# Latent attention: the queries without rotary part by rows, ahead of the rotary ones, through a DRAM round trip

## The chip, the cores and the metric

One Trainium2 chip, one core of it. The metric is the device time of one execution of the whole program in microseconds; the time before is the median of three runs.

## What is computed

A decoder trunk of four layers on 256 tokens of width 2048, all in float32. Layers 0 and 3 mix tokens by latent attention, layer 1 by sparse attention, layer 2 by a sliding window. Every layer also attends to a memory and multiplies its heads by a SiLU gate. The change touches only the latent layers. Cut to what it touches:

```python
c_q, c_kv, k_rope, mq, gate = _split(h @ w_in, [1536, 512, 64, 1024, 3072])
q  = (_rmsnorm(c_q, q_norm) @ w_uq).reshape(B, S, 16, 128 + 64)
kv = (_rmsnorm(c_kv, kv_norm) @ w_ukv).reshape(B, S, 16, 128 + 128)
q_nope, q_rope = q[..., :128], _rope(q[..., 128:])
k_nope, v = kv[..., :128], kv[..., 128:]
s = (einsum('bqhd,bkhd->bhqk', q_nope, k_nope) + einsum('bqhd,bkd->bhqk', q_rope, _rope(k_rope))) * scale
p = softmax(where(causal, s, -1e30))
o = einsum('bhqk,bkhd->bqhd', p, v)
```

## The kernel before

Products keep float32 accuracy by splitting both factors into a high and a low part (`split`, `parts_of`) and adding three products: high by high, high by low, low by high. ScalarE writes the high part `wh`, VectorE subtracts and writes the low part `wl`; each has three buffers, the raw weights `wr` five, so that weights are split up to two stages ahead of the one that TensorE is using.

There are two forms of projection. `columns_by` holds the weights still and streams the tokens, so that features come out on the partitions: per 128 input features and 256 output features it issues two matmuls of 512 columns and two of 256. `rows_by` holds the tokens still and streams the weights, so that tokens come out on the partitions: per 128 input features and up to 512 output features it issues six matmuls of that many columns. What `rows_by` gives must still be transposed before it can be a factor of the scores. `turned` transposes 32x32 blocks on VectorE, `stored` writes the result to DRAM with one DMA, and `fetched` reads it back with four DMAs that put the blocks in their places; `placed` is the two together, on GpSimd's queue.

A latent layer works in parts. Part 4 is memory heads, then parts 0 to 3 are four heads each, then part 5 is memory heads again. For each of parts 0 to 3 `Latent.project` forms, in this order on TensorE: the rotary queries by rows (`acc_qr`), the queries without rotary part by columns in two halves (`acc_qn`), the keys by columns in two halves (`acc_kn`) and the values by rows (`acc_va`). The rotary queries go from PSUM through `rope` and `turned` into the round trip (`qrT`, `placed`, `qrR`), and are split into two stacked parts (lines 832 and 833) when they are back. The others are split straight out of PSUM by `head_parts`. Then `attend` computes the scores of four heads (`sp`), `gate_by_rows` the gate (`acc_gr`), and `w_out` the output projection of the part before (`acc_wo`). There are eight such parts in the program.

The program is built with `schedule_with_timeline_sim=True`: the order of the instructions in each engine's queue is fixed when it is built, by a list schedule over modelled times, and may differ from the order in the text. `keep_in_program_order(ins)` pins one instruction behind the one traced just before it on its engine. The copy of what a round trip brings back is pinned in this way each time. On the chip every engine works through its queue in order and waits at the first instruction whose inputs are not there.

Tiles share buffers by tag. `pq` has five buffers; a part takes five tiles of it (`qrR`, two `qn`, two `kn`). PSUM has two accumulators `acc` and four small banks `mp`.

Of the kernel before, what the change touches and what calls it, by code (L numbers as in the profile page):

```python
# [8 lines left out]
F32 = mybir.dt.float32  # L9
# [6 lines left out]
P = 128  # L16
# [16 lines left out]
def kernel(ctx: ExitStack, tc: tile.TileContext, a: dict, out: bass.AP,  # L33
# [13 lines left out]
    def tmp(name, n=512, dt=F32):  # L47
        return wk.tile([P, n], dt, name=name, tag=f"t{n}", bufs=3)
# [5 lines left out]
    def f32(ap):  # L54
        return ap.bitcast(F32)

    def copy_act(o, i, scale=1.0):
        return nc.scalar.activation(o, i, AF.Copy, scale=scale)  # L58

    def split(hi, lo, src):  # L60
        copy_act(hi, src)
        nc.vector.tensor_sub(lo, src, f32(hi))  # L62
# [181 lines left out]
    def rows_by(xt, kts, w, k0, cols, name, hooks={}, opening=False, between={}):  # L244

        acc = accumulators(name)
        n = cols[1] if len(cols) == 2 else cols[1] * cols[4]
        step = 4 if n <= 256 else ST
        for s in range(0, kts, step):
            wr, n = stage(w, k0 + s, step, cols)  # L250
            if opening:
                for f in hooks[s]:
                    f()
            wh, wl = parts_of(wr, step * n, n if opening and s < 8 else None)
            with ExitStack() as held:
                for f in between.get(s, ()):
                    ins = f()
                    if ins is not None:
                        held.enter_context(tc.issue_after(ins))
                for k in range(step):  # L260
                    q = xt[(s + k) // 4]
                    at = slice(k * n, (k + 1) * n)
                    for t in range(2):
                        xh, xl = (q[:, v, (s + k) % 4, t * P:(t + 1) * P] for v in range(2))
                        first, last = s + k == 0, s + k == kts - 1
                        nc.tensor.matmul(acc[:, t, :n], xh, wh[:, at], start=first, stop=False)  # L266
                        nc.tensor.matmul(acc[:, t, :n], xh, wl[:, at], start=False, stop=False)  # L267
                        nc.tensor.matmul(acc[:, t, :n], xl, wh[:, at], start=False, stop=last)  # L268
            for f in () if opening else hooks.get(s, ()):
                f()  # L270
        return acc

    def columns_by(xt, kts, w, k0, cols, name, hooks={}, apart=False):

        if apart:
            acc = [misc(f"acc_{name}")[:].rearrange("p (v s) -> p v s", v=2) for j in range(2)]
        else:
            whole = accumulators(name)[:].rearrange("p j (v s) -> p j v s", v=2)
            acc = [whole[:, j] for j in range(2)]
        step = 2 * ST  # L280
        for s in range(0, kts, step):
            wr, n = stage(w, k0 + s, step, cols)
            wh, wl = parts_of(wr, step * n)
            for k in range(step):
                kt = s + k
                q = xt[kt // 4]
                first, last = kt == 0, kt == kts - 1
                at = [slice(k * S + j * P, k * S + (j + 1) * P) for j in range(2)]
                for j in range(2):
                    nc.tensor.matmul(acc[j], wh[:, at[j]], q[:, :, kt % 4, :], start=first, stop=False)  # L290
                for j in range(2):
                    nc.tensor.matmul(acc[j][:, 0, :], wl[:, at[j]], q[:, 0, kt % 4, :],  # L292
                                     start=False, stop=last)
            for f in hooks.get(s, ()):
                f()
        return acc if apart else whole
# [169 lines left out]
    def placed(raw, T, n):  # L466
        fetched(raw, stored(T), n, nc.gpsimd.dma_start)
# [12 lines left out]
    def quads(q):  # L480
        return q.rearrange("p m (t b) -> p m t b", b=32)

    def raw_tile(name):
        return act.tile([P, 1024], F32, name=name, tag="pq", bufs=PQ)
# [249 lines left out]
    class Latent:  # L734
# [76 lines left out]
        def project(self, g, steps):  # L811

            j = self.j
            wq, wkv = a["w_uq"][j], a["w_ukv"][j]
            qn, kn = [], []
            qr = act.tile([P, 4, S], F32R, name="qrT", tag="aux", bufs=AUX)
            v = [act.tile([P, 2, 512], F32R, name="va", tag="aux", bufs=AUX) for z in range(2)]
            acc = rows_by(self.cT[:3], 12, wq, 0, (g * 768, 4, 192, A_NOPE, A_ROPE), "qr",
                          {0: steps[:1], 4: steps[1:3], 8: steps[3:]})
            T, raw = tmp("qrT")[:].rearrange("p (t w) -> p t w", t=2), raw_tile("qrR")  # L820
            for t in range(2):
                rr = wk.tile([P, 4, A_ROPE], F32, name="qrr", tag="e", bufs=4)
                rope(rr, acc[:, t, :S].rearrange("p (h d) -> p h d", h=4), t, 4)
                turned(T[:, t], rr.rearrange("p h d -> p (h d)"), 2)
            placed(raw[:].rearrange("p (t w) -> p t w", t=8), T, 2)
            for half in range(2):
                acc = columns_by(self.cT[:3], 12, wq, 0, (g * 768 + half * 384, 2, 192, 0, A_NOPE), "qn")
                q = act.tile([P, 2, 2, S], F32R, name="qn", tag="pq", bufs=PQ)
                head_parts(q, acc)
                qn.append(q)  # L830
            r4 = raw[:].rearrange("p (t m b) -> p m t b", m=4, b=32)
            tc.keep_in_program_order(copy_act(quads(qr), r4))
            nc.vector.tensor_sub(quads(qr)[64:], r4[64:], quads(f32(qr))[64:])
            for half in range(2):
                acc = columns_by(self.cT[3:], 4, wkv, 0, (g * 1024 + half * 512, 2, 256, 0, A_NOPE), "kn",
                                 apart=half == 1)
                k = act.tile([P, 2, 2, S], F32R, name="kn", tag="pq", bufs=PQ)
                head_parts(k, acc)
                kn.append(k)
            acc = rows_by(self.cT[3:], 4, wkv, 0, (g * 1024, 4, 256, A_NOPE, A_NOPE), "va")  # L840
            split(v[0], v[1], acc)
            return (qn, qr, kn, v), lambda: gate_by_rows(self.nm, self.w, self.g0 + g * 512)

        def attend(self, qn, qr, kn, v):
            ws = []
            for h in range(4):
                def score(b):
                    sp = misc("sp")
                    qs = slice(b * P, (b + 1) * P)
                    q, k, z = qn[h // 2], kn[h // 2], h % 2  # L850
                    if b == 0:
                        seq = [(q[:, 0, z, qs], k[:, :, z, :P]), (q[:, 1, z, qs], k[:, :, z, :P]),
                               (qr[:, h, qs], self.kr[:, :, :P])]
                    else:
                        seq = [(q[:, 0, z, qs], k[:, 0, z, :]), (q[:, 0, z, qs], k[:, 1, z, :]),
                               (q[:, 1, z, qs], k[:, 0, z, :]),
                               (qr[:, h, qs], self.kr[:, 0, :]), (qr[:, h, qs], self.kr[:, 1, :])]
                    for n_, (l, r_) in enumerate(seq):
                        nc.tensor.matmul(sp[:, :S], l, r_, start=n_ == 0, stop=n_ == len(seq) - 1)
                    return sp  # L860
                if h % 2 == 0:
                    ws.append(Turn(2, CAUSAL))
                ws[-1].add(h % 2, masked_softmax(score, lambda b, n, u: caus[:, S - n:], self.scale))
                if h % 2 == 1:
                    ws[-1].send()

            def sums(z, y, gT, p_s):
                o = misc("o")
                pp = [p_.rearrange("p (t n b) -> p t n b", t=12, n=2) for p_ in p_s[0]]
                for s in range(2):  # L870
                    c = (2 * z + s) * P
                    for t in range(2):
                        ts = slice(8 * t, 8 + 4 * t)
                        for n_, (u, p_) in enumerate(((0, 0), (0, 1), (1, 0))):
                            nc.tensor.matmul(o[:, s * S + t * P:(s + 1) * S], v[u][:, t, c:c + P],
                                             pp[p_][:, ts, s, :], start=t == n_ == 0, stop=t == 1 and n_ == 2)
                return None, lambda: gated(y, o, gT, 2 * z)
            return Sums([ws[:1], ws[1:]], sums)
# [408 lines left out]
```

## Time and profile before

| | |
|---|---|
| runs, median (lowest to highest) | 2529.37 us (2529.0 to 2533.69) |
| profiled execution, its own time | 2527.35 us |
| its span in the trace | 2525.6 us |
| TensorE busy (PE) | 2507.0 us, 99% |
| VectorE (DVE), ScalarE (ACT), GpSimd (POOL) busy | 72%, 56%, 15% |
| mean granted TensorE clock | 0.999 |

PE is TensorE's matmuls, PEld its weight loads, which overlap them. DMA-issuing instructions are not counted as busy time. A matmul's row gives its start and the time until its result is written; matmuls overlap, so the pace is read from the starts.

### The profile page before, as it was taken

The page shows a single profiled execution, that of the slowest core. Times are in us where ns is not written, and L with a number is a line of the kernel's source. Part 1 is how long each engine was busy: PE and PEld are TensorE (multiplying, and loading weights), DVE is VectorE, ACT ScalarE, POOL GpSimd, SP SyncE. Part 2 cuts the span into 40 slices and gives each one's busy share as a digit, 9 for nine tenths or more (in the row PEclk, how much of TensorE's full clock was granted, in tenths as well). Part 3 has the DMA queues.
Part 4 walks back from the last instruction along what each step waited for, and adds up shares of the span by engine and source line. Part 5 has one row for each costly group of instructions (what it writes and reads, how often), then busy time and mean ns, then how long its engine had stood idle before and what let it go on. Part 6 is the DMA issues. An engine that isn't in the chain of part 4 may idle for free.

```text
span 2525.6 us, 37537 instructions
## 1 busy us (share of the span) xinstructions
PE 2507.0 (99%) x13076; PEld 2150.6 (85%) x13076; DVE 1809.3 (72%) x3047; ACT 1417.7 (56%) x2228; POOL 367.6 (15%) x585
## 2 busy tenths in 40 slices
PE   8999999999999999999999999999999999999998
PEld 6888888888888888988888888888889898888887
DVE  6555556677777675778888775888877667767677
ACT  6454545554555555566666555666665655545554
POOL 1000000111121100012222201222220011111210
PEclk9999999999999999999999999999999999999999
DMA  9888888778778756679989677999975877788874
GB/s 315 264 281 291 268 262 243 211 202 211 216 223 227 212 189 193 199 240 275 261 276 266 208 217 207 271 271 270 258 232 165 241 195 212 208 223 225 244 206 148
DMA packets 462014, 588.85 MB, mean 233 GB/s; under 512 B 78896, under 2 KB 294592, under 8 KB 460672
## 3 DMA queue, kind: packets, MB, share of 16 engines
q1 hardware_dynamic: 424080, 470.76, 63.5%
q0 software_dynamic: 36736, 114.78, 15.7%
q8 instruction: 103, 1.69, 0.3%
q10 hardware_dynamic: 1008, 0.91, 0.1%
q14 instruction: 87, 0.71, 0.1%
HBM read 532.10 MB, written 66.81 MB: 237 GB/s over the span
## 4 chain that ended last, share of the span: by engine, by line
PE 97%; DMA 1%; DVE 1%; ACT 1%; issue 0%; POOL 0%; SPq 0%; ACTq 0%; DVEq 0%; POOLq 0%
PE acc_mq L290 5%; PE acc_g L290 5%; PE acc_gr L266 5%; PE acc_gr L267 5%; PE acc_gr L268 5%; PE acc_wo L268 4%; PE acc_wo L267 4%; PE acc_wo L266 4%; PE acc_cq L290 4%; PE acc_qn L290 3%; PE acc_wo L241 3%; PE acc_wo L239 3%; PE acc_wo L240 3%; PE acc_mq L292 2%; PE acc_g L292 2%; PE acc_mk L267 2%
## 5 line engine op out<-in xcount | busy, mean ns | idle before, releaser
L72 DVE TENSOR_TENSOR wl<-wr,wh 128x1024 fp32r<-128x1024 f32 (+2 forms) x860 | 1027.9, 1197 | 556.0 <-ACT wh L58 542.5
L58 ACT ACTIVATE wh<-wr 128x1024 fp32r<-128x1024 f32 (+2 forms) x860 | 891.3, 1038 | 845.3 <-PE acc_gr L268 96.9
L266 PE MATMUL acc_gr<-wh,xT 128*128 128x512 f32 x512 | 199.7, 390 | 0.0
L267 PE MATMUL acc_gr<-wl,xT 128*128 128x512 f32 x512 | 199.6, 390 | 0.0
L268 PE MATMUL acc_gr<-wh,xT 128*128 128x512 f32 x512 | 199.4, 390 | 0.0
L266 PE MATMUL acc_wo<-wh,y 128*128 128x512 f32 x432 | 168.7, 390 | 0.0
L267 PE MATMUL acc_wo<-wl,y 128*128 128x512 f32 x432 | 168.6, 390 | 0.0
L268 PE MATMUL acc_wo<-wh,y 128*128 128x512 f32 x432 | 168.6, 390 | 0.0
L290 PE MATMUL acc_g<-xT,wh 128*128 128x512 f32 x512 | 162.1, 395 | 0.0
L290 PE MATMUL acc_mq<-xT,wh 128*128 128x512 f32 x512 | 161.9, 396 | 0.0
L577 POOL DMA_DIRECT2D pL<-turn x192 | 120.3, 633 | 195.4 <-DMA turn<-T 86.7
L241 PE MATMUL acc_wo<-wh,y 128*128 128x512 f32 x320 | 125.0, 391 | 0.2 <-DVE y L62 0.2
L239 PE MATMUL acc_wo<-wh,y 128*128 128x512 f32 x320 | 124.9, 390 | 0.0
L240 PE MATMUL acc_wo<-wl,y 128*128 128x512 f32 x320 | 124.8, 390 | 0.0
L1191 DVE TENSOR_TENSOR x<-x,acc_wo 128x1024 f32<-128x1024 f32 x92 | 111.5, 1212 | 16.0 <-PE acc_wo L268 11.8
L572 POOL DMA_DIRECT2D turn<-T x56 | 42.8, 765 | 539.6 <-DVE T L566 472.0
L290 PE MATMUL acc_qn<-cT,wh 128*128 128x512 f32 x384 | 120.6, 395 | 0.0
L290 PE MATMUL acc_cq<-xT,wh 128*128 128x512 f32 x384 | 120.6, 395 | 0.0
L292 PEld LDWEIGHTS acc_g<-xT,wl 128*128 128x128 f32 x512 | 96.0, 188 | 21.7
L292 PEld LDWEIGHTS acc_mq<-xT,wl 128*128 128x128 f32 x512 | 95.2, 188 | 21.2
L268 PEld LDWEIGHTS acc_gr<-wh,xT 128*128 128x128 f32 x512 | 96.2, 188 | 19.6
L266 PEld LDWEIGHTS acc_gr<-wh,xT 128*128 128x128 f32 x512 | 96.3, 188 | 18.8
(337 smaller groups left out, 5791.2 us busy)
## 6 DMA issues: line engine op xcount, KB each, us to landing
wr<-in_w_out_dram SPq DMA_DIRECT2D x192, 512.0 KB, 4.8
wr<-in_w_in_a_dram SPq DMA_DIRECT2D x176, 512.0 KB, 4.6
wr<-in_w_mem_kv_dram SPq DMA_DIRECT2D x128, 512.0 KB, 5.8
wr<-in_w_in_b_dram SPq DMA_DIRECT2D x116, 512.0 KB, 4.7
wr<-in_w_in_c_dram SPq DMA_DIRECT2D x104, 512.0 KB, 5.0
wr<-in_w_uq_dram SPq DMA_DIRECT2D x288, 128.0 KB, 3.7
turn<-T POOLq DMA_DIRECT2D x40, 384.0 KB, 5.0
tab<-flat POOLq DMA_DIRECT2D x8, 1536.0 KB, 11.4
```

What stands on the lines that cost most here:

```text
L58: return nc.scalar.activation(o, i, AF.Copy, scale=scale)
L72: two = nc.vector.tensor_sub(lo, src, f32(hi))
L239: nc.tensor.matmul(accs[c][:, t], xh, wh[:, at], start=first, stop=False)
L240: nc.tensor.matmul(accs[c][:, t], xh, wl[:, at], start=False, stop=False)
L241: nc.tensor.matmul(accs[c][:, t], xl, wh[:, at], start=False, stop=last)
L266: nc.tensor.matmul(acc[:, t, :n], xh, wh[:, at], start=first, stop=False)
L267: nc.tensor.matmul(acc[:, t, :n], xh, wl[:, at], start=False, stop=False)
L268: nc.tensor.matmul(acc[:, t, :n], xl, wh[:, at], start=False, stop=last)
L290: nc.tensor.matmul(acc[j], wh[:, at[j]], q[:, :, kt % 4, :], start=first, stop=False)
L292: nc.tensor.matmul(acc[j][:, 0, :], wl[:, at[j]], q[:, 0, kt % 4, :], start=False, stop=last)
L577: nc.gpsimd.dma_start(f32(self.raw)[j * 32:(j + 1) * 32, :].rearrange("p (i r) -> p i r", r=r), bass.AP(tensor=d.tensor, offset=d.offset + ...
L1191: nc.vector.tensor_add(xs, xs, acc)
```

## The change

In each of the eight parts the queries without rotary part are formed first, by `rows_by` with 512 output features. ScalarE copies them out of PSUM, VectorE transposes them in blocks, and they make the same round trip through DRAM that the rotary queries make. Then come the rotary queries, the keys and the values. The split of the fetched queries (`parts_q`) is traced inside the value projection, that of the rotary queries behind it. The scores read the two parts from two tiles instead of one; their matmuls are the same in number and size. A part now takes seven tiles of tag `pq`, which still has five buffers.

```diff
-            acc = rows_by(self.cT[:3], 12, wq, 0, (g * 768, 4, 192, A_NOPE, A_ROPE), "qr",
+            acc = rows_by(self.cT[:3], 12, wq, 0, (g * 768, 4, 192, 0, A_NOPE), "qn",
                           {0: steps[:1], 4: steps[1:3], 8: steps[3:]})
+            T, qraw = act.tile([P, 2, 512], F32, name="qnT", tag="pq", bufs=PQ), raw_tile("qnR")
+            for t in range(2):
+                rows_ = wk.tile([P, 512], F32, name="qnz", tag="z", bufs=2)
+                copy_act(rows_, acc[:, t])
+                turned(T[:, t], rows_, 4)
+            placed(qraw[:].rearrange("p (t w) -> p t w", t=8), T, 4)
+            acc = rows_by(self.cT[:3], 12, wq, 0, (g * 768, 4, 192, A_NOPE, A_ROPE), "qr")
...
             for half in range(2):
-                acc = columns_by(self.cT[:3], 12, wq, 0, (g * 768 + half * 384, 2, 192, 0, A_NOPE), "qn")
-                q = act.tile([P, 2, 2, S], F32R, name="qn", tag="pq", bufs=PQ)
-                head_parts(q, acc)
-                qn.append(q)
-            r4 = raw[:].rearrange("p (t m b) -> p m t b", m=4, b=32)
-            tc.keep_in_program_order(copy_act(quads(qr), r4))
-            nc.vector.tensor_sub(quads(qr)[64:], r4[64:], quads(f32(qr))[64:])
-            for half in range(2):
                 acc = columns_by(self.cT[3:], 4, wkv, 0, (g * 1024 + half * 512, 2, 256, 0, A_NOPE), "kn",
                                  apart=half == 1)
                 k = act.tile([P, 2, 2, S], F32R, name="kn", tag="pq", bufs=PQ)
                 head_parts(k, acc)
                 kn.append(k)
-            acc = rows_by(self.cT[3:], 4, wkv, 0, (g * 1024, 4, 256, A_NOPE, A_NOPE), "va")
+
+            def parts_q():
+                q = [act.tile([P, 4, S], F32R, name="qn", tag="pq", bufs=PQ) for z in range(2)]
+                r4 = qraw[:].rearrange("p (t m b) -> p m t b", m=4, b=32)
+                tc.keep_in_program_order(copy_act(quads(q[0]), r4))
+                nc.vector.tensor_sub(quads(q[1]), r4, quads(f32(q[0])))
+                qn.extend(q)
+            acc = rows_by(self.cT[3:], 4, wkv, 0, (g * 1024, 4, 256, A_NOPE, A_NOPE), "va", {0: [parts_q]})
             split(v[0], v[1], acc)
+            r4 = raw[:].rearrange("p (t m b) -> p m t b", m=4, b=32)
+            tc.keep_in_program_order(copy_act(quads(qr), r4))
+            nc.vector.tensor_sub(quads(qr)[64:], r4[64:], quads(f32(qr))[64:])
```

## Rows read from the trace of the kernel before

**Rows 1.** The page: its span, and TensorE's busy time.

```profile
span 2525.6 us, 37537 instructions
...
PE 2507.0 (99%) x13076; PEld 2150.6 (85%) x13076; DVE 1809.3 (72%) x3047; ACT 1417.7 (56%) x2228; POOL 367.6 (15%) x585
```

**Rows 2.** Waits of PE: total us, times, longest.

```profile
PE acc_mv L266 <- ACT wh L58: 7.4, 1, 7.4
PE acc_mv L267 <- DVE wl L72: 1.4, 2, 0.7
PE acc_va L266 <- DVE qn L317: 1.1, 2, 0.7
```

**Rows 3.** Timeline of PE, first latent part: start, us, instruction.

```profile
502.83 0.28 PE L266 MATMUL acc_qr<-wh,cT 128*128 128x256 f32 x1
...
511.58 0.63 PE L290 MATMUL acc_qn<-cT,wh 128*128 128x512 f32 x2
...
524.79 0.62 PE L290 MATMUL acc_qn<-cT,wh 128*128 128x512 f32 x2
...
531.06 0.63 PE L290 MATMUL acc_kn<-cT,wh 128*128 128x512 f32 x2
...
536.63 0.40 PE L266 MATMUL acc_va<-wh,cT 128*128 128x512 f32 x1
...
542.10 0.40 PE L859 MATMUL sp<-kn,qn 128*128 128x256 f32 x2
...
557.13 0.39 PE L267 MATMUL acc_gr<-wl,xT 128*128 128x512 f32 x1
...
567.78 0.39 PE L239 MATMUL acc_wo<-wh,y 128*128 128x512 f32 x1
```

**Rows 4.** Tile acc_qn, on DVE: duration ns, least, median, most.

```profile
L317 DVE TENSOR_TENSOR qn<-zl,acc_qn x16: 677/687/689, 524.9 to 2366.1; 128x512 fp32r<-128x512 f32 x16
```

**Rows 5.** Tiles gTt and qrT: the operations nearest to the added ones.

```profile
L457 DVE STREAM_TRANSPOSE gTt<-th x32: 669/705/711, 573.1 to 2406.0; 128x512 f32<-128x512 f32 x32
...
L58 ACT ACTIVATE qrT<-qrR x8: 1051/1052/1061, 532.5 to 2363.7; 128x1024 fp32r<-128x1024 f32 x8
L833 DVE TENSOR_TENSOR qrT<-qrR,qrT x8: 1222/1223/1224, 534.0 to 2364.8; 64x1024 fp32r<-64x1024 f32 x8
```

**Rows 6.** DMA issues: count, KB each, median us from issue to landing.

```profile
qrR<-placed POOLq DMA_DIRECT2D x32, 128.0 KB, 5.4
...
placed<-qrT POOLq DMA_DIRECT2D x8, 256.0 KB, 3.5
...
placed<-ckT POOLq DMA_DIRECT2D x2, 512.0 KB, 5.3
```

**Rows 7.** Timelines of DVE and POOL, first part: the rotary queries' way out.

```profile
516.45 0.45 DVE L457 STREAM_TRANSPOSE qrT<-qrr 128x256 f32<-128x256 f32 x1
...
517.20 0.72 POOL L463 DMA_DIRECT2D placed<-qrT  x1 [17.79 <-DVE qrT L457]
520.75 2.33 POOL L473 DMA_DIRECT2D qrR<-placed  x4 [2.84 <-issue]
```

**Rows 8.** Timelines of ACT, first part, and waits of ACT.

```profile
542.30 1.03 ACT L58 ACTIVATE va<-acc_va 128x1024 fp32r<-128x1024 f32 x1 [1.66 <-PE acc_va L268]
...
ACT wh L58 <- PE acc_gr L268: 96.9, 74, 1.7
```

**Rows 9.** Tile qrT's waits, and POOL, ACT, PE in the second part.

```profile
  DMA qrR<-placed: 3.8, 3
...
612.72 2.42 POOL L473 DMA_DIRECT2D qrR<-placed  x4 [4.68 <-DMA placed<-qrT]
...
620.92 1.06 ACT L58 ACTIVATE qrT<-qrR 128x1024 fp32r<-128x1024 f32 x1 [1.70 <-DMA qrR<-placed]
...
624.10 0.47 PE L266 MATMUL acc_va<-wh,cT 128*128 128x512 f32 x1 [0.65 <-DVE qn L317]
```

**Rows 10.** Timelines of DVE and PE: the attention sums of one part.

```profile
583.82 0.95 DVE L585 TENSOR_TENSOR pL<-pL,pH 128x768 fp32r<-128x768 f32 x1
...
589.72 0.28 PE L875 MATMUL o<-pL,va 128*128 128x256 f32 x1
```

More of the change, by code (lines that the diff above doesn't have):

```diff
@@ L849, in score @@
                     qs = slice(b * P, (b + 1) * P)
-                    q, k, z = qn[h // 2], kn[h // 2], h % 2
+                    (hi, lo), k, z = (u[:, h, qs] for u in qn), kn[h // 2], h % 2
                     if b == 0:
-                        seq = [(q[:, 0, z, qs], k[:, :, z, :P]), (q[:, 1, z, qs], k[:, :, z, :P]),
+                        seq = [(hi, k[:, :, z, :P]), (lo, k[:, :, z, :P]),
                                (qr[:, h, qs], self.kr[:, :, :P])]
                     else:
-                        seq = [(q[:, 0, z, qs], k[:, 0, z, :]), (q[:, 0, z, qs], k[:, 1, z, :]),
-                               (q[:, 1, z, qs], k[:, 0, z, :]),
+                        seq = [(hi, k[:, 0, z, :]), (hi, k[:, 1, z, :]), (lo, k[:, 0, z, :]),
                                (qr[:, h, qs], self.kr[:, 0, :]), (qr[:, h, qs], self.kr[:, 1, :])]
```

## The prediction

> **What bounds the kernel now.** I read the page first, then the waits of TensorE, then the timelines of one latent part. The page shows TensorE busy for 2507.0 of 2525.6 us [rows 1], and the list of its waits shows hardly anything else: 8.8 us in the projection of the memory values, and 1.1 us in two of the eight latent parts [rows 2]. So time can go in two ways only: TensorE is given less work, or it is made to wait. VectorE, ScalarE, GpSimd and the DMA queues matter only through the second.
>
> **What TensorE saves.** I compare the two forms by the distance of their matmuls' starts. By columns, nine blocks of 128 input features for 256 outputs lie between 524.79 and 531.06 us, which is 0.697 us for each [rows 3]. By rows, 47 matmuls of 512 columns lie between 557.13 and 567.78 us, 0.2266 us for each [rows 3]. A part needs 24 blocks by columns, 24 x 0.697 = 16.72 us, or 12 x 6 = 72 matmuls by rows, 72 x 0.2266 = 16.32 us. That is 0.40 us in a part and 3.2 us in eight. The columns streamed are the same; 96 matmuls become 72. The first matmuls of the value projection are slower, 5.47 us for 24 between 536.63 and 542.10 [rows 3], which is 0.228 each; at that pace the saving would be 0.30 a part, 2.4 us. I take 3.2, since before and behind the new stage stands work that is as steady as the gate's, and keep 2.4 as its lower end.
>
> The 1.1 us wait [rows 2] also goes: the value projection waited for an accumulator that `head_parts` on VectorE had not yet emptied, and the accumulator that it takes is now the rotary queries', which `rope` has read before the last transpose ends, 5.3 us behind `acc_qr` [rows 7]; the keys between take 5.57 [rows 3]. Together 4.3 us off 2527.35.
>
> **What costs nothing.** VectorE gives up two subtractions and two additions of 0.69 us a part [rows 4], 2.7 us, and takes on two transposes of 0.70 and one subtraction that I price at the 1.22 us of the rotary one [rows 5], 2.6 us. ScalarE takes on one copy of 1.05 us [rows 5], 8.4 us in all at 56% busy. GpSimd issues five more DMAs a part, at the 0.72 and 2.33 us of the rotary ones [rows 7], 24 us in all at 15% busy. 8 MB more pass through DMA. The weights come in 12 larger loads instead of 24. All of it lies under TensorE's 99%. If that cover were gone, only ScalarE's 8.4 us and GpSimd's 24 us would show.
>
> **What becomes late.** Before, the rotary queries' round trip ran under the whole `acc_qn` stage: from the end of `acc_qr` at 511.58 to the first score at 542.10 are 30.5 us [rows 3]. After, only keys and values lie between: 531.06 to 542.10, 11.0 us [rows 3]. Does the round trip fit?
>
> Counted from the end of `acc_qr`: the second transpose ends at 516.90, +5.3; the store is issued at +5.6 and the fetches from +9.2 [rows 7]. They are four, of 0.58 us each, so the last starts at +10.9, and lands 5.4 us later by the median [rows 6], at +16.3. ScalarE's copy takes 1.05 and VectorE's subtraction 1.22 [rows 5]; with 0.3 us for the two hand-overs the scores can start at +18.9. That is 7.9 us behind the end of the value projection. The second part gives the late side: there the fetches came 0.72 + 4.68 = 5.4 us after the store's start, against 3.6 in the first part, and ScalarE waited for the last of them until 620.92, 8.2 us after 612.72 [rows 9], against my 7.1. That makes 5.6 + 5.4 + 8.2 + 2.6 = +21.8, 10.8 us behind.
>
> On ScalarE the copy stands pinned behind the copy of the values, which ends 1.2 us behind the value projection [rows 3, 8], at +12.3. From there to +16.3 ScalarE waits, and behind it in its queue stand the splits of the gate's next weights. TensorE lives on the weights that are already split. With three buffers and one in use these are two stages, 24 matmuls of 0.2266, 5.4 us. That buffers are what splits wait for, not ScalarE, shows in its waits: 97 us, in 74 pieces, for a gate stage to end [rows 8]. So TensorE runs dry for 7.9 - 5.4 = 2.4 us in each part, 19 us in eight parts. The ends of this term: nothing, if a third gate stage is split in time (8.2 us of cover); (10.8 - 5.4) x 8 = 43 us, if all parts are like the second; 63 us, if the scores were queued directly behind the values, 7.9 x 8.
>
> That a late landing reaches TensorE through ScalarE's queue, the trace shows on a small scale. In three of eight parts the copy waited for the fetch, 3.8 us together; where it waited 1.70 us, TensorE lost 0.65 at the next accumulator, in spite of the longer distance [rows 9].
>
> There is one more coupling. Seven tiles share five `pq` buffers. While the fetched queries, both keys and the two query parts live, all five are taken, so the rotary fetch may have to wait until the subtraction of `parts_q` has freed the fetched tile. Out of PSUM by an estimated +2.5 us behind `acc_qn` (two copies of half of 1.05, a last transpose of 0.70 and hand-overs, from [rows 5]), stored by +7.8 and landed by +15 [rows 6, 7], split by +17.6: with 8.75 us for `acc_qr` between [rows 3], +8.8 on the rotary count, just ahead of +9.2. It adds nothing in the middle case and belongs to the late end.
>
> The sum: 2527.35 - 4.3 + 19 = 2542. The runs' median lies 2.0 us above the profiled execution, so I forecast 2544 us for the median.
>
> **The rivals.** First, the round trip stays hidden. The order of the queue is chosen over modelled times, and TensorE is often given an operand later than it is there: one attention sum starts 5 us after its subtraction has ended [rows 10]. If the scores are queued behind three gate stages or more, and the third stage's split stands ahead of the waiting copy, TensorE never waits and only the saving is left: 2529.4 - 4.3 = 2525. Against it stands that the copy is pinned so that ScalarE arrives at it 4 us too early, however well the rest is ordered.
>
> A rule speaks for this rival. The Trainium skill, page "DMA: Bandwidth & Descriptors", section "Anatomy of one DMA — SWDGE (gpsimd) path", gives a DMA from GpSimd's queue as 2.0 us plus its bytes at 436 GB/s; that would be an estimated 2.6 us for the store and 2.3 for a fetch, data at about +12.5, just when ScalarE comes to it, and a sum of 2525. The trace's medians of 3.5 and 5.4 [rows 6] speak against it.
>
> Second, the queries without rotary part are late as well. `parts_q` is pinned behind the split of the value projection's first weights only. If ScalarE reaches it before the fetch lands at +15, the split of the value projection's second weights waits behind it: 15 + 1.05 + 1.05 + 1.2 = 18.3, where TensorE wants them at 8.75 + 5.57 + 2.73 = 17.0 after `acc_qn` [rows 3, 5]. This adds 1.3 us a part, 10 us in all: 2554. It decides only if that split is not yet made when `acc_kn`'s first half ends.
>
> Third, the scores are queued directly behind the values: 2529 - 4.3 + 63 = 2588. In the trace before they are, but there their inputs were long there.
>
> **How the numbers follow.** A measurement of this kernel can tell about 0.2%, 5 us, from no change. I give 0.52 to the forecast, of which 0.12 is for stalls of under 9 us in all, which would leave the time within 5 us; 0.36 to the first rival; 0.08 to the second; 0.04 to the third. The first rival's 2525 lies 0.8 us from the line of 2524.3, so a good third of it, 0.13, counts as faster and 0.23 as the same. Slower is 0.40 + 0.08 + 0.04 = 0.52, the same 0.12 + 0.23 = 0.35. The forecast's own range, with stalls of 1 to 4.5 us a part, is 2533 to 2561. The range takes in the first rival, down to 2523, and reaches up to 2566, 5 us a part, short of the late end and the third rival.
>
> **What would show it.** Right: `acc_qn` by rows takes 16.3 us a part; ScalarE's list of waits has the rotary copy behind its fetch with 2 to 6 us each, eight times; TensorE's list has `sp` or `acc_gr` with 1 to 4 us each, behind that copy, its subtraction or a weight split. Wrong: no new wait of TensorE, with several gate matmuls between the values and the first score; or waits in `acc_va`, which would be the second rival. The forecast fails if the modelled order leaves 8 us or more of gate work ahead of the first score.

## The result, and the profile after

The changed kernel takes 2549.22 us in the median of four runs (2544.14 to 2551.99), the kernel before 2529.78 beside it: a ratio of 1.0068, 95% interval 1.0055 to 1.0081. By that ratio it is 17 us slower; 2544 was forecast. The profiled execution of the changed kernel took 2544.14 us, with a span of 2542.4, against 2525.6 [rows 1]: 16.8 us more.

The page: span, and busy time of each engine.

```profile
span 2542.4 us, 37010 instructions
...
PE 2509.7 (99%) x12884; PEld 2141.5 (84%) x12884; DVE 1805.0 (71%) x3039; ACT 1419.5 (56%) x2236; POOL 392.0 (15%) x625
```

The waits of PE, which answer to [rows 2] (total us, times, longest):

```profile
PE sp L867 <- DVE kn L317: 13.1, 8, 1.6
PE acc_mv L266 <- ACT wh L58: 7.1, 1, 7.1
PE acc_mv L267 <- DVE wl L72: 1.4, 2, 0.7
PE o L883 <- ACT pH L58: 1.1, 1, 1.1
PE sp L867 <- DVE qn L844: 0.6, 2, 0.4
```

and of ACT and DVE:

```profile
ACT qrT L58 <- DMA qrR<-placed: 39.0, 8, 5.6
...
DVE qrT L850 <- ACT qrT L58: 30.1, 8, 4.5
```

ACT waits for the rotary fetch eight times, 4.9 us on average, as forecast. But PE's new wait stands elsewhere: at the first scores, for the low part of the *keys*. Of what hangs on the rotary fetch, PE's list has only 0.6 us.

The second latent part shows why. The timeline of PE, then ACT, DVE and POOL (start, us, instruction):

```profile
625.54 0.40 PE L266 MATMUL acc_va<-wh,cT 128*128 128x512 f32 x1
...
630.79 0.39 PE L268 MATMUL acc_va<-wh,cT 128*128 128x512 f32 x1
632.81 0.59 PE L867 MATMUL sp<-kn,qn 128*128 128x256 f32 x3 [1.64 <-DVE kn L317]
...
641.81 0.39 PE L266 MATMUL acc_gr<-wh,xT 128*128 128x512 f32 x1
642.62 0.39 PE L867 MATMUL sp<-kn,qn 128*128 128x256 f32 x1 [0.42 <-DVE qn L844]
```

```profile
628.49 1.06 ACT L58 ACTIVATE wh<-wr 128x1024 fp32r<-128x1024 f32 x1 [1.92 <-PE acc_va L268]
629.46 1.12 ACT L58 ACTIVATE kn<-acc_kn 128x512 fp32r<-128x512 f32 x3
...
632.31 1.08 ACT L58 ACTIVATE wh<-wr 128x1024 fp32r<-128x1024 f32 x1
638.99 1.06 ACT L58 ACTIVATE qrT<-qrR 128x1024 fp32r<-128x1024 f32 x1 [5.60 <-DMA qrR<-placed]
...
631.99 0.68 DVE L317 TENSOR_TENSOR kn<-zl,acc_kn 128x512 fp32r<-128x512 f32 x1
...
640.08 1.22 DVE L850 TENSOR_TENSOR qrT<-qrR,qrT 64x1024 fp32r<-64x1024 f32 x1 [4.49 <-ACT qrT L58]
641.34 1.23 DVE L844 TENSOR_TENSOR qn<-qnR,qn 128x1024 fp32r<-128x1024 f32 x1
...
626.16 0.72 POOL L463 DMA_DIRECT2D placed<-qrT  x1 [5.68 <-DVE qrT L457]
630.44 2.46 POOL L473 DMA_DIRECT2D qrR<-placed  x4 [3.56 <-ACT kn L58]
```

The keys are complete in PSUM when the values begin, at 625.54. ACT copies them out at 629.46 only, behind a split of gate weights that itself waits 1.92 us for a buffer. Their low part comes at 632.67 and the first scores at 632.81; the values end at 631.02 (their last start and one pace of 0.2266). That is 1.8 us in each of the eight parts, 14.3 us. Before, the first copy of the keys started 6.8 to 7.3 us ahead of the values' end; now it starts 1.6 ahead. In the kernel before, in the first part, where the values end at 542.10:

```profile
534.78 0.58 ACT L58 ACTIVATE kn<-acc_kn 128x512 fp32r<-128x512 f32 x1
```

The first scores need no rotary part and no low part of the queries. The matmuls that do stand 9.3 us behind the first scores, after 37 gate matmuls (8.4 us) and a few more scores, so the late rotary data (copied from 8.0 us behind the values' end on, split by +10.3) cost little. POOL's row names the keys' copy as what released the fetch, but it is only the last of several: from the store's issue to the first fetch it is 4.3 to 7.2 us in the eight parts, and 3.7 to 7.0 in a later run (`e_aux`) in which the keys are copied much earlier. The last two rows of DVE show a second thing to explain: the low part of the queries without rotary part (L844), whose data were copied to their high part at 630.46, is formed at 641.34, right behind the rotary subtraction (L850).

### The profile page after: what moved, and what is told of

Read it like the earlier page. It is cut to its first block, busy times and chain, and to the rows that moved or that the text cites. A ratio compares the mean times of both kernels' runs of the same rounds, so it can differ in the third digit from the quotient of the medians.

```text
span 2542.4 us, 37010 instructions
## 1 busy us (share of the span) xinstructions
PE 2509.7 (99%) x12884; PEld 2141.5 (84%) x12884; DVE 1805.0 (71%) x3039; ACT 1419.5 (56%) x2236; POOL 392.0 (15%) x625
## 5 line engine op out<-in xcount | busy, mean ns | idle before, releaser
L267 PEld LDWEIGHTS acc_gr<-wl,xT 128*128 128x128 f32 x512 | 96.3, 188 | 18.5
```

## The experiments

Two theories at first. *Rotary*, the prediction's: the fetch is late, and what stands behind it sets the loss. *Keys*: the late copy of the keys is the loss. Times are medians; a ratio is to the kernel before on the same chip. Times "behind the values" are counted from the last `acc_va` matmul's start and one pace.

**The changed kernel again** (`after_again`).

> The changed kernel once more, as the measure for the other three, which run on the same chip. Every theory: 2544 to 2552 us. The profile again shows in each of the 8 parts a gap of about 1.8 us on PE ahead of the first scores (first use of the keys' low part), and ACT waiting some 5 us for the fetch of the rotary queries 8 times.

2550.33 us, ratio 1.0083 (1.0071 to 1.0095). The 13.1 us at the keys come back to the digit. This profiled execution, 2552.00 us, has 5 us more of waits of PE at the attention sums (`o` behind `pH`, the high part of the probabilities) than the first: the 10 us between its runs lie at least partly there.

**Keys first** (`e_kn`). The gate's stages are built inside `issue_after` of the keys' copies.

```diff
+ def gating():
+     with ExitStack() as held:
+         for ins in keys_first:      # head_parts' copies out of PSUM
+             held.enter_context(tc.issue_after(ins))
+         return gate_by_rows(...)
```

> One order is changed: ACT issues the copies of the gate's stages only behind the two copies of the keys out of PSUM. The gap of 1.8 us ahead of the first scores (keys' low part) must go in any case. The keys theory (the late copy of the keys is the loss, 8 x 1.8 = 14 us of it): 2528 to 2534 us, with no new wait on PE. The rotary theory (the prediction's: rotary parts and, in the queue behind them, the queries' low parts are ready some 11.5 us behind the values, and the cover is about 10 us without the gap): the gap moves to the first matmul with the queries' low part, 1 to 2 us in each part, and the time stays at 2538 to 2548 us.

2578.93 us, 1.0197 (1.0174 to 1.0219): worse than either theory said. The gap at the keys is gone. PE's waits now, and the timelines of ACT and PE in the second part:

```profile
PE acc_gr L266 <- ACT wh L58: 15.0, 8, 2.9
PE acc_gr L267 <- DVE wl L72: 8.4, 8, 1.1
```

```profile
643.54 1.06 ACT L58 ACTIVATE qrT<-qrR 128x1024 fp32r<-128x1024 f32 x1 [7.32 <-DMA qrR<-placed]
644.50 2.94 ACT L58 ACTIVATE wh<-wr 128x1024 fp32r<-128x1024 f32 x3
...
645.60 0.49 PE L266 MATMUL acc_gr<-wh,xT 128*128 128x512 f32 x1 [2.47 <-ACT wh L58]
```

This is the prediction's mechanism: ACT stands at the rotary copy, three weight splits stand behind it, PE runs dry, though behind three gate stages (36 matmuls) and not two. In the changed kernel the gap at the keys hides it: there, in the second part, the fourth gate stage starts at 641.81 and its split ends at about 641.0, so without the 1.8 us PE would have been there 1.0 us too early. The keys theory, taken alone, falls.

**No wait for the rotary fetch** (`e_rot`).

```diff
- r4 = raw[:].rearrange("p (t m b) -> p m t b", m=4, b=32)    # ahead of the split into qr
+ r4 = qraw[:].rearrange("p (t m b) -> p m t b", m=4, b=32)
```

> The split of the rotary queries reads the tile of the queries without rotary part instead of the fetched one, so that no engine waits for the rotary fetch; all instructions and transfers stay, and the output has wrong rotary queries (that part of the computation is left out). The rotary theory: ACT's 8 waits of 5 us go, and with them the spread and most of the loss: 2526 to 2532 us. The keys theory: the gap of 1.8 us ahead of the first scores stays in each of the 8 parts, and the time stays at 2540 to 2548 us.

2542.53 us, 1.0055 (1.0043 to 1.0067), 7.8 below `after_again`. The keys' 13.1 us stay. So the rotary wait on ACT is worth 3 to 8 us (against 1.0068 and 1.0083), and most of the loss is not it.

**Both** (`e_both`).

> Both edits: the keys' copies ahead of the gate's on ACT, and no wait for the rotary fetch (rotary queries left out as in the run before it). Every theory that names only these two waits: 2523 to 2529 us, which is the kernel before less the 3 to 4 us that queries formed in rows save. If it stays above 2535 us, a third cause, the round trip of the queries without rotary part or the shared buffers, has to be looked for.

2573.02 us, 1.0177 (1.0164 to 1.019). A third cause, then. PE's waits, and the timelines of DVE and PE in the second part:

```profile
PE sp L877 <- DVE qn L849: 22.0, 7, 3.8
```

```profile
640.53 1.23 DVE L849 TENSOR_TENSOR qn<-qnR,qn 128x1024 fp32r<-128x1024 f32 x1 [5.42 <-DMA qrR<-placed]
...
641.81 0.74 PE L877 MATMUL sp<-kn,qn 128*128 128x256 f32 x4 [2.61 <-DVE qn L849]
```

In this kernel nothing reads the fetched rotary queries. Yet the subtraction that forms the low part of the *other* queries waits 5.42 us until that fetch has landed (in `e_rot` it already waits for it, 14.1 us in eight parts). It reads `qnR` and writes `qn`; the reading that fits is that the tile which it writes gets the buffer of `qrR`. Seven tiles share five buffers of `pq`, and the last of the part takes the place of the rotary data. A third theory, *buffers*: this coupling, and what the build makes of it in the order of ACT and PE.

**One tile out of the shared pool** (`e_aux`). `aux` has four buffers, of which a part takes three.

```diff
- raw = raw_tile("qrR")                                              # tag "pq"
+ raw = act.tile([P, 1024], F32, name="qrR", tag="aux", bufs=AUX)
```

> One tile is moved: the fetched rotary queries (qrR) lie in the pool of qrT and va (aux, four buffers, three used so far in a part) and no longer in the shared pool pq. The low part of the queries without rotary part then has a buffer of its own and need not wait until the rotary fetch has landed and been split. The buffers theory (the five pq buffers hold the low part back, and with it the order on ACT and PE that follows): 2525 to 2534 us, the gap of 1.8 us ahead of the first scores gone or below 0.7, no PE wait for the queries' low part. The rotary theory (the fetch is late by itself, ACT's queue stands behind it): ACT still waits some 5 us 8 times, PE runs dry behind it, 2538 to 2548 us.

2534.51 us, 1.0011 (1.0002 to 1.0019), against 1.0068 and 1.0083: most of the loss is gone with one tag, though the time is 0.5 us above the range of the buffers theory. The rotary fetch is as late as ever, and ACT still waits for it, 25.0 us in eight parts. But the keys' copy is back at its old place, the subtraction of the queries' low part starts 1.6 to 2.7 us *ahead* of the values' end, and PE has no wait at the scores. Its waits, and the timelines of ACT and PE in the second part, where the values end at 629.14:

```profile
PE acc_mv L266 <- ACT wh L58: 7.6, 1, 7.6
PE o L883 <- ACT pH L58: 3.6, 2, 2.3
PE acc_mv L267 <- DVE wl L72: 1.4, 2, 0.7
```

```profile
621.82 0.58 ACT L58 ACTIVATE kn<-acc_kn 128x512 fp32r<-128x512 f32 x1
...
632.68 1.06 ACT L58 ACTIVATE wh<-wr 128x1024 fp32r<-128x1024 f32 x1 [1.36 <-PE acc_gr L268]
638.34 1.06 ACT L58 ACTIVATE qrT<-qrR 128x1024 fp32r<-128x1024 f32 x1 [4.60 <-DMA qrR<-placed]
...
629.37 0.52 PE L867 MATMUL sp<-kn,qn 128*128 128x256 f32 x3
...
640.71 0.98 PE L867 MATMUL sp<-kr,qrT 128*128 128x256 f32 x6
```

The first rotary scores of this part stand 11.6 us behind the values, and the split rotary queries are there 11.5 us behind: just in time. The move changed more than the keys' place. In all eight parts a fourth gate stage is now split ahead of the rotary copy, 3.5 us behind the values' end (632.68 here); the changed kernel has three there, the last at +1.3 (632.31 in its rows above). So ACT's wait for the rotary fetch now stands behind more finished weights. Which of the three, the keys' copies, the free low part or the fourth split, is worth how much was not taken apart.

**The tile moved and the keys first** (`e_auxkn`).

> The tile moved as in the run before it, and the keys' copies ahead of the gate's on ACT, which made 2579 us when the tile was not moved. The buffers theory: with both the stalls on the queries' low part and on the gate's copies go, 2524 to 2532 us. The rotary theory: PE waits for the gate's copies behind ACT's rotary wait as without the move, 2560 to 2580 us.

2537.2 us, 1.0026 (1.0016 to 1.0036), against 1.0197 for the same order without the move. That order is not bad by itself. What differs on ACT is again the fourth gate split: it stands ahead of the rotary copy in every part here, behind it in `e_kn`. The time is 5 us above the range of the buffers theory, and far below that of the rotary one.

**The order alone** (`e_order`): the kernel before, its `acc_qn` halves moved ahead of `acc_qr`, the rotary split moved behind the values.

```diff
+ for half in range(2): acc = columns_by(..., "qn"); ...; qn.append(q)
  acc = rows_by(..., "qr", ...)
- for half in range(2): acc = columns_by(..., "qn"); ...; qn.append(q)
- (copy and subtraction of the rotary queries)
  ...
  split(v[0], v[1], acc)
+ (copy and subtraction of the rotary queries)
```

> The kernel before with the order of the change alone: queries without rotary part first, still formed by columns and split straight from PSUM, the rotary ones second, their split behind the values. No second round trip, and no more tiles in pq than before. The rotary theory: the rotary fetch lands as late as in the changed kernel, 2538 to 2550 us. The buffers theory: the rotary scores stand far enough back, 2527 to 2533 us, as before, with ACT waiting some us at the rotary copy and nothing behind it.

2544.94 us, 1.0061 (1.0049 to 1.0074): nearly the whole loss, without a second round trip and with five tiles in five buffers. PE's list:

```profile
PE sp L859 <- DVE kn L317: 13.1, 8, 1.6
```

The same 13.1 us, at the keys, not at the rotary scores. The rotary theory's time came out, by another wait than it names; the buffers theory, as a matter of counting buffers, missed.

**The form alone** (`e_form`): rotary queries first, split ahead of the values; the others second, by rows and with the round trip, split behind the values.

```diff
+ acc = rows_by(..., A_NOPE, A_ROPE), "qr", ...); ...; placed(raw, T, 2)
  acc = rows_by(..., 0, A_NOPE), "qn"); ...; placed(qraw, T, 4)
- acc = rows_by(..., A_NOPE, A_ROPE), "qr"); ...; placed(raw, T, 2)
  (the keys)
+ (copy and subtraction of the rotary queries)
  (the values, without parts_q)
  split(v[0], v[1], acc)
- (copy and subtraction of the rotary queries)
+ parts_q()
```

> The form of the change alone: rotary queries first and split ahead of the values as before, queries without rotary part second, by rows and with the round trip, split behind the values. Their data land some 3.5 us behind the values' end by the trace of the changed kernel (16.5 us behind their last matmul), their parts are ready some 6 to 7 us behind it, and some 25 gate matmuls (5.7 us) are put ahead of their scores. The rotary theory: nothing rotary is late, so most of the loss goes: 2526 to 2534 us. If the second round trip itself is the loss wherever it stands: 2540 us and more.

2533.64 us, 1.0011 (1.0002 to 1.002). PE waits at the scores once, 3.4 us, in the last part. So the new form and its round trip cost nothing that matters; the order does. Here, too, seven tiles share five buffers with the rotary queries among them, but these land 8.7 us or more ahead of the values' end: without the late fetch, sharing the pool did no harm here.

**The order alone, with the tile moved** (`e_orderaux`): the edit of `e_aux` in `e_order`.

> The order of the change alone (queries by columns and first, rotary ones second and split behind the values, 2545 us) with the fetched rotary queries moved out of pq into aux, as in the run that brought the changed kernel to 2534.5 us. If sharing pq is what puts the keys' copies late on ACT: the 8 gaps of 1.8 us ahead of the first scores go, 2528 to 2534 us. If the late rotary fetch by itself is the loss: 2540 us and more.

2535.98 us, 1.0023 (1.0012 to 1.0034), down from 1.0061. The eight waits at the keys are gone from PE's list; one of 2.1 us at the rotary scores of the last part is new. The time is 2 us above the range given for the shared pool, but well below 2540.

**Six buffers** (`e_six`), and its control (`e_wr4`).

```diff
- PQ, AUX, WR = 5, 4, 5
+ PQ, AUX, WR = 6, 4, 4    # control: the kernel before with 5, 4, 4
```

> The changed kernel with six pq buffers for five; to make room, the staged weights have four for five. The queries' low part has a buffer of its own again, but the fetched rotary queries stay in pq with the keys. If the number of buffers is the cause: 2527 to 2534 us, beside its control. If it is the sharing of the pool with the rotary fetch: the 8 gaps of 1.8 us ahead of the first scores stay (13 us), 2538 to 2546 us.

> The control of the run with six buffers: the kernel before with four buffers for the staged weights and nothing else. Every theory: within 3 us of the kernel before if a fourth buffer ahead suffices; what it loses is taken off the run with six.

2556.47 us, 1.0106 (1.0093 to 1.012), and 2543.77 for the control, 1.0051 (1.0037 to 1.0065). The control is not within 3 us: the fifth buffer of raw weights is worth 13 us. What six buffers leave of the change is 2556.47 - 2543.77 = 12.7 us, and PE's list in this run has

```profile
PE sp L867 <- DVE kn L317: 13.4, 8, 1.9
```

The subtraction of the queries' low part now starts 1.6 to 2.2 us behind the values, not 9 to 10, and this uncoupling saves an estimated 4 to 8 us (12.7 against 17 and 21, the ratios of the changed kernel), if the cost of the missing weight buffer simply adds, which no run shows. The keys are as late as before. So there are two effects of the one shared pool: the low part bound to the rotary buffer, which a sixth buffer cures, and the keys' place in ACT's queue, which it does not, while taking `qrR` out of the pool cures both.

**The kernel before, again** (`before_again`).

> The kernel before, a second profile of it. Between the values' ends of the fourth and the fifth part (stages that the change does not touch) the first profile has 1308.8 us and the changed kernels 1311.5 to 1314.2 us. If that difference is run to run, this profile has a value between them; if the change reaches into those stages, 1309 us again.

2529.17 us. The last `acc_va` matmuls of the fourth and the fifth part, here and in `e_aux`:

```profile
803.01 0.39 PE L268 MATMUL acc_va<-wh,cT 128*128 128x512 f32 x1
...
2111.83 0.39 PE L268 MATMUL acc_va<-wh,cT 128*128 128x512 f32 x1
```

```profile
801.92 0.39 PE L268 MATMUL acc_va<-wh,cT 128*128 128x512 f32 x1
...
2115.80 0.39 PE L268 MATMUL acc_va<-wh,cT 128*128 128x512 f32 x1
```

1308.8 us again, against 1313.9. Every kernel with the new order or form is longer there, by 2.7 us (the first profile of the changed kernel) to 6.9 (`e_both`). But this stretch is not free of the change, as the expectation has it: it begins with the scores and attention sums of the fourth part and ends with the query stages of the fifth. In the changed kernel 1.8 of the 2.7 us are the fourth part's gap at the keys.

## Why the prediction came out as it did

The time, the side and the size were right; the largest term, the 19 us, was put at the wrong wait, so the size is in part luck.

*What TensorE saves.* In the first part the two query stages go from 503.76 to 531.64 us, 27.88 against 28.23 [rows 3]: 0.35 a part, between the 0.40 taken and the 0.30 kept as lower end. Free of stalls the saving shows in the distance of whole parts. From the first to the fourth values' end it is 260.9 us before, 260.1 in `e_aux` and 259.1 in `e_form`; but the 260.9 hold a wait of 0.65 at `acc_va`. Where neither kernel waits, a part is 86.65 us before (third to fourth values' end), 86.40 in `e_aux` and 86.37 in `e_form`: 0.25 to 0.3 less, so the lower end, 2.4 us in all, is the better figure. The wait of 1.1 us at `acc_va` is gone from PE's list.

*What costs nothing.* Right: DVE, ACT and POOL are busy for 71, 56 and 15%, POOL for 24.4 us more (24 forecast), and `e_form`, which has all of the added work, loses 0.1%.

*What becomes late.* The rotary data are late by what was worked out. The fetches start at -0.6 to +2.3 us against the values' end, the copy at +6.6 to +8.0, and the split is ready by +9 to +10.3; +7.9 was the middle and +10.8 the late case. ACT's eight waits of 4.9 us were forecast as 2 to 6. The Trainium skill, page "DMA: Bandwidth & Descriptors", section "Anatomy of one DMA — SWDGE (gpsimd) path", would have had a fetch land within an estimated 2.3 us; the medians after are 4.8 us (`qrR`) and 5.0 (`qnR`), beside the 5.4 of [rows 6], so the trace speaks against it a second time.

*The step that failed: how much work covers it, and what comes first.* The sum set the stall as 7.9 - 5.4 us: of three weight buffers one was counted as in use, which left two gate stages. In the trace a third stage is split in every part at +1.3 us, behind the copy of the values and ahead of the rotary copy, for the last values' buffer is free by then. That is the end of the term which the prediction put at nothing, a third gate stage split in time. The queue has part of the scores directly behind the values, since they need no rotary part, and 37 gate matmuls, 8.4 us, ahead of those that do. The condition that the prediction gave for its failure, 8 us or more of gate work, was thus met for the scores that count. In the changed kernel the rotary term is 0.6 us on PE's list and 3 to 8 us by `e_rot`, not 19. In its place stand 14.3 us at the keys, which no step of the prediction named: its account of ACT's queue stopped at the splits of weights and did not ask where the copies of the keys would go. That the forecast 19 us and these are near each other is chance, except in this: both come from ACT's queue, and `e_kn` shows the forecast stall at the forecast place (23.4 us, ACT's rotary wait and three splits behind it) as soon as the keys' gap is removed.

*The buffers.* "It adds nothing in the middle case" was wrong. The prediction looked at whether the coupling delays the *fetch*. It delays the low part of the queries, whose tile follows the rotary data in the same buffer. What decides is wider than that: with the rotary tile in the keys' pool and its fetch late, the build puts the keys' copies late, in `e_order` even with five tiles in five buffers. One tile moved to another tag takes the ratio from 1.0068 or 1.0083 to 1.0011.

*The rivals.* The first, all hidden, is what `e_aux` nearly is: hidden with 11.6 us of cover, as that rival asked for, but at 2534.5 and not 2525. The second, queries without rotary part late, did not come about through `acc_va`, which has no wait. The third did not happen: directly behind the values stand only scores that need no rotary part.

*What stays open.* In the profiled executions, `e_aux` is 4.8 us over the kernel before: -0.8 and -1.1 between the parts' values' ends in the two groups of four parts, +5.1 in the stretch between, +1.7 behind the last. The 5.1 us are no run-to-run matter, since the second profile of the kernel before has 1308.8 again. Of them 4.1 arise between 49 and 71 us behind the fourth values' end, in that part's own attention sums: PE stops there for `pH`, and the granted clock falls behind the stop.

```profile
860.40 0.39 PE L883 MATMUL o<-pH,va 128*128 128x256 f32 x1 [2.29 <-ACT pH L58]
...
862.00:866.00 4.00, 4.00 (x20) 3.78 (x19) 2.59 (x4) 1.54 (x3) 0.00 (x0) 0.61 0.54 147
```

Another 1.3 us arise in later layers whose text is the same (0.7 of it is `acc_wo` behind `x`), and the fifth part's queries by rows give 0.35 back. In `e_form`, which has no such stop, most of the 4.7 us arise in those later layers. Why the order changes there was not settled. Nor was the rule by which the build puts the keys' copies late and the fourth gate split behind the rotary copy when the rotary tile shares the keys' pool; shown is that moving the tile moves them, in two kernels. No version was found that beats the kernel before: without stalls some 3 to 4 us are to be had (2.0 to 2.8 of TensorE's work and the wait of 1.1), and the best runs of `e_aux` (2527.65) and of the kernel before on that chip (2527.65) are equal.

## What to carry to other kernels

A change that puts a longer-lived tile into a shared pool couples whatever takes that buffer next; ask for each added tile which instruction will write into its place, and what that one feeds. When an order in a queue is chosen by a list schedule, the wait that shows is only the first of several: remove it and look what is next before calling it the cause, as `e_kn` cost 29 us by curing 13. And move data that wait for a slow transfer into a pool of their own before adding buffers to the one that they block.

## What the runs showed of the hardware

Behind some of PE's stops its clock fell. In `e_both`, PE stood from about 639.0 to 641.8 us in the second part. The matmuls of 512 columns that follow start 0.43 us apart instead of 0.2266, until 646.1 us. The windows ahead of the stop, behind it, and later (us, busy times, PEclk third from the end):

```profile
630.00:638.80 8.80, 8.80 (x43) 7.38 (x42) 3.59 (x3) 5.25 (x6) 2.33 (x4) 1.00 0.71 201
641.80:646.40 4.60, 4.19 (x12) 3.34 (x13) 4.54 (x4) 0.00 (x0) 0.00 (x0) 0.63 0.39 114
646.50:655.00 8.50, 8.50 (x46) 7.28 (x45) 6.09 (x28) 5.47 (x13) 0.00 (x0) 1.00 0.58 196
```

The granted clock went to the lower of its two levels, 1.2 of 2.4 GHz, for 3 to 4 us. How long PE stood does not by itself tell whether this happens. Behind the stop of 2.3 us in `e_aux` (860.40, above) the clock fell too. Behind the 1.8 us gaps of the changed kernel it stayed at 1.00, and so it did behind a stop of 3.6 us in the last part of `e_form`:

```profile
632.80:637.40 4.60, 4.59 (x22) 3.88 (x23) 2.79 (x4) 0.59 (x1) 0.10 (x1) 1.00 0.81 205
...
2383.39 0.97 PE L869 MATMUL sp<-kn,qn 128*128 128x256 f32 x6 [3.40 <-ACT qn L58]
...
2383.40:2387.40 4.00, 4.00 (x22) 3.52 (x23) 3.50 (x4) 2.32 (x3) 2.33 (x4) 1.00 0.41 107
```

Over the whole run the mean is 0.992 in `e_both` and 0.993 in `e_kn`, against 0.998 to 0.999 in the others except `e_six` (0.997). PE's busy time is 2524.7 us in `e_both` and 2509.7 in the changed kernel, 15.0 more for the same matmuls. PE's list in `e_both` has 27.3 us at `sp` and `acc_gr`, the changed kernel's 14.8 at `sp` and `o`. The 15.0 us and the 12.5 between the lists make up the 26.8 us between the spans, within 0.7.
